# Sums for the seven-product form: x halves summed early, weights summed by transfers and one item ahead

## The chip, the cores and the metric

The kernel runs on one core of one Trainium2 chip. The metric is the device time of one execution in microseconds (us).

## The reference

Two decoder layers on a residual stream of 256 tokens by 2048, all in float32. Each layer has an attention, a cross attention into 256 memory tokens, and an MLP. Layer 0 uses differential attention; it is the stage that the change mostly touches.

```python
for i in range(DEPTH):                       # DEPTH = 2
    h = rms_norm(x, attn_norm[i])
    if i % 2 == 0:
        x = x + diff_attention(h, da_wqkv, da_lambda, da_subln, da_wo, cos_p, sin_p, lambda_init)
    else:
        x = x + mla_attention(h, ...)
    x = x + memory_cross_attention(rms_norm(x, cross_norm[i]), mem_h, ca_wq[i], ca_wkv[i], ca_wo[i])
    x = x + sq_relu_mlp(rms_norm(x, mlp_norm[i]), mlp_wup[i], mlp_wdown[i])   # square(relu(h @ wup)) @ wdown
return rms_norm(x, final_norm)

# diff_attention: q, k, v = split(h @ wqkv); q and k are rotated (cos, sin) in the first
# quarter of each head; per head two softmaxes p0, p1, a = p0 - lam * p1, o = a @ v
```

## The kernel before

**Products in halves.** Every float32 operand is split into a high part (the value rounded to the matmul's format) and a low part (value minus high part), and a product takes three matmuls: high·high, high·low, low·high. For the weights this happens on the fly. `load` brings 1 MB into a raw tile of 128x2048 (pool `wraw`, 7 slots) through SP's DMA queue. `split_pieces.next` then makes, for each half of the tile, `whi` by a cast on ScalarE (line 195) and `wlo` by a subtract on VectorE (line 196). The pool of these halves holds two raw tiles' worth, so a cast waits until TensorE has freed a slot. TensorE works on one half-tile of an ordinary item with 12 matmuls of 128x512, and so on through the list `plan`. `fill` keeps AHEAD = 4 items split ahead of `take`, and calls the `begin` of the next item already when it splits the one before. `hooks[n]` are run at the n-th `take`.

**The order** of the instructions on each engine is set by a scheduler with a cost model, within what is kept in program order (the queues, and the token "weights" on VectorE's splits and weight sums).

**Seven products.** Three of the query/key chunks of the diff layer (the groups 1 to 3, one class `Seven` for each in `diff_line`) and 14 blocks of the MLP (7 per layer, in `mlp_line`) multiply a 2x2 block matrix by a 2x2 block matrix in seven products p1 to p7 instead of eight. For it sums are needed on both sides. On the side of x these are s1 to s4 of x's quarters (`Forms.sums_of`, line 427 for the sum, `halves` at lines 396 and 397 for its high and low part). On the side of the weights they are built in the raw tiles, for each product in two halves x = 0, 1 of 1 MB:

- p5's tile is p1's tile plus block (0,1), by an add on VectorE (line 791) when p5's item begins.
- p7's tile is the tile of block (0,1) plus p3's tile (block (1,1)), by an add on VectorE (line 800) right behind p3's split.
- p6's tile is p7's plus block (0,0), and p4's is p6's plus block (1,0). Both are made by a transfer that accumulates, on POOL's queue (line 804), issued behind the split of the one before.

**The diff layer's start.** The first 8 items are the q and k chunks of group 0, of 24 matmuls per half tile. `x_pieces` (hooks 2 to 5) and the first loads make the high and low parts `acts` of the scaled x transposed. After q and k, `heads_T` evicts the results to `ev` tiles (line 486), rotates them on POOL with the tables `cos` and `sin` (lines 497 to 502), and TensorE transposes them (`mm<-identr,ev`, line 159). The tables are made on VectorE and ScalarE (lines 1006 to 1020). Only then `GivenForms` reads xT again (four transfers into two raw tiles), scales it on ScalarE (line 459), and makes the sums s1 to s4 for the products of the groups. Beside each group's products run the values' chunk, the output projection of the group before, and the attention of the group before as background tasks: `nmax` (541), `rsum` (548, 668), and `a` (674, 675) are parts of its softmax on VectorE.

Of the kernel before, what the change touches and what calls it, by code (L numbers as in the profile page):

```python
# [14 lines left out]
ALU = mybir.AluOpType  # L15
# [30 lines left out]
def trunk(ctx, tc, x, xT, mem, memT, positions, gcols, gfinal, lam_vecs, consts, W, out):  # L46
# [329 lines left out]
    class Forms(Stream):  # L376
# [37 lines left out]
        def sums(self):  # L414
            for key in [(t, h) for t in range(NT) for h in range(2)]:
                for task in self.forms[key].tasks:
                    yield task
            for x in range(2):
                self.sums_of(x, *(self.raw[t][:, 8 * h + 4 * x : 8 * h + 4 * x + 4] for t in range(NT) for h in range(2)))
                yield T_TURN  # L420

        def sums_of(self, x, a11, a12, a21, a22):
            for key, o, p, q, op in (
                ("s1", a22, a21, a22, ALU.subtract), ("s3", a21, a11, a21, ALU.subtract),
                ("s2", a22, a22, a11, ALU.subtract), ("s4", a12, a12, a22, ALU.add),
            ):
                nc.vector.tensor_tensor(o, p, q, op)  # L427
# [13 lines left out]
    class GivenForms(Forms):  # L441


        def __init__(self, src, units, gcol):
            self.src, self.units, self.gcol = src, units, gcol
            self.forms = {}
            task = Task(self.sums())
            for key in ("s1", "s2", "s3", "s4"):
                self.form(key).tasks.append(task)

        def sums(self):
            for x in range(2):
                rows = raw_tile().rearrange("p (k t) -> p k t", t=S)
                for h in range(2):
                    u = 2 * h + x
                    load(rows[:, 4 * h : 4 * h + 4], self.src[:, 4 * u : 4 * u + 4, :])
                    for i in range(4):
                        row = rows[:, 4 * h + i]
                        nc.scalar.activation(row, row, AF.Copy, scale=g[:, self.gcol + 4 * u + i : self.gcol + 4 * u + i + 1])
                    yield T_TURN  # L460
                self.sums_of(x, *(rows[:, 4 * h : 4 * h + 4, t * P : (t + 1) * P] for t in range(NT) for h in range(2)))
                yield T_SM

        def pieces(self, key):
            if key in self.forms:
# [297 lines left out]
    class Seven:  # L763
# [15 lines left out]
        def fetch(self, i, j, x):  # L779
            raw = raw_tile()  # L780
            load(raw, self.source(i, j, x))
            return raw

        def job(self, p, x):
            def begin():
                r = self.raw
                if p in self.B:
                    r[p, x] = self.fetch(*self.B[p], x)
                if p == "p5":
                    r[p, x], r["p7", x] = r["p1", x], self.fetch(0, 1, x)  # L790
                    in_turn(nc.vector.tensor_tensor(r[p, x], r[p, x], r["p7", x], ALU.add))  # L791

            def run():
                o = self.raw[p, x]
                split = split_pieces(o, 4 * CH, 2)
                for _ in range(2):
                    split.next()
                if p == "p3":
                    r = self.raw
                    in_turn(nc.vector.tensor_tensor(r["p7", x], r["p7", x], o, ALU.add))  # L800
                if p in self.ADDED:
                    after, block = self.ADDED[p]
                    self.raw[after, x] = o
                    add = nc.gpsimd.dma_start(o, self.source(*block, x), accum_op=ALU.add)  # L804
                    tc.keep_in_program_order(add)
                return split.halves

            run.begin = begin
            return run

        def items(self):
# [2 lines left out]
        def products(self, a, u, copied, out):  # L814
# [724 lines left out]
```

## Time and profile before

| | |
|---|---|
| median of 3 runs | 2243.6 us (2242.57 to 2243.88) |
| the profiled execution | 2243.97 us, its span 2242.1 us |
| TensorE busy | 2213.5 us, 99% of the span |
| VectorE, ScalarE, POOL busy | 1751.3, 1422.6, 185.3 us |
| mean granted clock of TensorE | 0.996 |
| matmuls | 10449 |

PE is TensorE (PEld its weight loads), DVE VectorE, ACT ScalarE, POOL GpSimd, SP the engine whose queue issues the loads. A row of a timeline gives start and duration in us, the engine, the line of the kernel, the operation, what it writes and reads, how many stand in the row, and in brackets the idle time ahead of it and what ended it. A row of the waits gives the sum, the number and the longest. A row of the windows gives for each engine the busy time and the number of instructions, then TensorE's granted clock, the share of the 16 DMA engines, and GB/s. q0 is the queue of POOL's transfers, q1 that of the others.

### The profile page before, as it was taken

What the parts mean: (1) busy time and instruction counts of PE and PEld (TensorE: products, weight loads), DVE (VectorE), ACT (ScalarE), POOL (GpSimd) and SP (SyncE); (2) the same over time, 40 slices, a digit from 0 to 9 for tenths busy, and PEclk for the clock granted to TensorE, in tenths of its full rate; (3) what the DMA queues carried; (4) which work ended last, traced back from release to release, by engine and by line L of the source; (5) the groups of instructions that cost most, each with busy time, mean ns of one, the idle gap of its engine ahead of it and who ended that gap; (6) DMA issues with size and microseconds to landing.
All of it is one profiled execution on the core that took longest, in us unless ns stands there. A gap on an engine that the chain in (4) does not pass through costs nothing.

```text
span 2242.1 us, 27565 instructions
## 1 busy us (share of the span) xinstructions
PE 2213.5 (99%) x10449; PEld 1841.6 (82%) x10449; DVE 1751.3 (78%) x1923; ACT 1422.6 (63%) x1921; POOL 185.3 (8%) x262
## 2 busy tenths in 40 slices
PE   9899999999999999999999999999999999999998
PEld 7678888888888888888889888888888888888886
DVE  6878888778888788788765766778887887887864
ACT  7766667666666666666655755566666666666664
POOL 0231120000000000000000311000000000000001
PEclk9999999999999999999999999999999999999999
DMA  9477787435887887877955234634679779779781
GB/s 381 159 238 227 238 241 257 164 132 208 258 257 242 253 257 241 252 255 235 274 171 186 102 141 160 253 132 151 235 236 274 242 234 276 241 235 274 238 291 57
DMA packets 75158, 498.78 MB, mean 222 GB/s; under 512 B 8592, under 2 KB 8976, under 8 KB 17680
## 3 DMA queue, kind: packets, MB, share of 16 engines
q1 hardware_dynamic: 64656, 424.66, 51.6%
q0 software_dynamic: 9792, 71.31, 16.8%
q8 instruction: 82, 1.34, 0.2%
q10 hardware_dynamic: 576, 1.05, 0.2%
q14 instruction: 52, 0.43, 0.0%
HBM read 494.88 MB, written 2.10 MB: 222 GB/s over the span
## 4 chain that ended last, share of the span: by engine, by line
PE 91%; DVE 5%; issue 1%; ACT 1%; DMA 1%; ACTq 0%; POOLq 0%; DVEq 0%
PE mm L155 61%; PE pr L155 23%; PE ax L155 3%; PE ax L159 2%; DVE wlo L196 2%; DVE raw L791 2%; ACT whi L195 1%; DMA raw<-in_da_wqkv_dram 1%; PE mm L159 1%; DVE unit L297 1%; DVE raw L800 0%; DVE unit L530 0%; DVE unit L397 0%; DVE raw L427 0%; DVE x L481 0%
## 5 line engine op out<-in xcount | busy, mean ns | idle before, releaser
L196 DVE TENSOR_TENSOR wlo<-raw,whi 128x1024 fp32r<-128x1024 f32 (+3 forms) x998 | 1199.0, 1211 | 411.1 <-ACT whi L195 374.7
L195 ACT CAST whi<-raw 128x1024 fp32r<-128x1024 f32 (+3 forms) x998 | 1038.5, 1042 | 692.8 <-PE mm L155 491.1
L155 PE MATMUL mm<-whi,unit 128*128 128x512 f32 (+3 forms) x4160 | 1324.0, 389 | 1.3 <-ACT unit L614 0.9
L155 PEld LDWEIGHTS mm<-whi,unit 128*128 128x128 f32 x4160 | 778.0, 188 | 153.4 <-ACT unit L614 1.3
L155 PE MATMUL mm<-wlo,unit 128*128 128x512 f32 (+3 forms) x2080 | 804.0, 387 | 6.5 <-DVE wlo L196 6.2
L155 PE MATMUL pr<-whi,unit 128*128 128x512 f32 x1904 | 614.2, 392 | 0.0
L155 PEld LDWEIGHTS mm<-wlo,unit 128*128 128x128 f32 x2080 | 391.8, 188 | 85.8 <-DVE wlo L196 14.4
L155 PEld LDWEIGHTS pr<-whi,unit 128*128 128x128 f32 x1904 | 358.6, 188 | 74.1
L155 PE MATMUL pr<-wlo,unit 128*128 128x512 f32 x952 | 372.3, 391 | 6.3 <-DVE wlo L196 6.1
L155 PEld LDWEIGHTS pr<-wlo,unit 128*128 128x128 f32 x952 | 179.4, 188 | 44.5 <-DVE wlo L196 8.3
L804 POOL DMA_DIRECT2D raw<-in_mlp_wup_dram x56 | 49.1, 876 | 1119.2 <-DVE wlo L196 1119.2
L481 DVE TENSOR_TENSOR x<-x,mm 128x512 f32<-128x512 f32 x152 | 99.8, 680 | 9.0 <-PE mm L155 8.5
L800 DVE TENSOR_TENSOR raw<-raw,raw 128x2048 f32<-128x2048 f32 x34 | 77.7, 2284 | 0.0
L791 DVE TENSOR_TENSOR raw<-raw,raw 128x2048 f32<-128x2048 f32 x34 | 77.6, 2283 | 0.0
L296 ACT CAST unit<-ax 128x512 fp32r<-128x512 f32 (+1 forms) x100 | 55.7, 570 | 26.1 <-PE ax L159 23.6
L336 POOL TENSOR_TENSOR rs<-rs,mhalf 128x1 f32<-128x1 f32 (+1 forms) x28 | 25.8, 925 | 556.0 <-DVE rs L335 556.0
L297 DVE TENSOR_TENSOR unit<-ax,unit 128x512 fp32r<-128x512 f32 (+1 forms) x100 | 65.3, 663 | 3.4 <-ACT unit L296 1.3
L543 ACT ACTIVATE p<-ax,nmax 128x256 f32<-128x256 f32 (+1 forms) x80 | 33.7, 429 | 24.7 <-DVE nmax L541 24.3
L330 ACT ACTIVATE junk<-x 128x512 bf16<-128x512 f32 x56 | 35.2, 628 | 9.4 <-DVE x L481 8.4
L155 PE MATMUL ax<-unit,unit 128*128 128x256 f32 (+1 forms) x240 | 37.2, 281 | 0.0
L155 PEld LDWEIGHTS ax<-unit,unit 128*128 128x128 f32 x240 | 34.3, 190 | 2.5
L155 PE MATMUL ax<-raw,unit 128*128 128x256 f32 (+1 forms) x240 | 35.3, 279 | 0.8 <-ACT unit L529 0.6
(182 smaller groups left out, 1020.9 us busy)
## 6 DMA issues: line engine op xcount, KB each, us to landing
raw<-in_mlp_wup_dram SPq DMA_DIRECT2D x128, 1024.0 KB, 5.0
raw<-in_mlp_wdown_dram SPq DMA_DIRECT2D x128, 1024.0 KB, 5.6
raw<-in_mlp_wup_dram POOLq DMA_DIRECT2D x56, 1024.0 KB, 9.3
raw<-in_da_wqkv_dram SPq DMA_DIRECT2D x45, 1024.0 KB, 7.0
raw<-in_da_wo_dram SPq DMA_DIRECT2D x16, 1024.0 KB, 5.5
raw<-in_ca_wkv_dram SPq DMA_DIRECT2D x16, 1024.0 KB, 5.0
raw<-in_mla_wo_dram SPq DMA_DIRECT2D x16, 1024.0 KB, 6.2
raw<-in_da_wqkv_dram POOLq DMA_DIRECT2D x12, 1024.0 KB, 11.0
```

What stands on the lines that cost most here:

```text
L155: return nc.tensor.matmul(o, stationary, moving, start=start, stop=stop, skip_group_check=not alone)
L159: nc.tensor.transpose(o, src, ident)
L195: nc.scalar.copy(hi, r)
L196: in_turn(nc.vector.tensor_tensor(lo, r, f32(hi), ALU.subtract))
L296: nc.scalar.copy(hi, src)
L297: nc.vector.tensor_tensor(dst[:, 1, :n, t * P : (t + 1) * P], src, f32(hi), ALU.subtract)
L330: nc.scalar.activation(junk[:, : src.shape[1]], src, AF.Square, accum_out=acc)
L481: nc.vector.tensor_tensor(xc, xc, ps, ALU.add)
L543: nc.scalar.activation(pr[:, i * w : (i + 1) * w], sb[:, i * w : (i + 1) * w], AF.Exp, bias=nmax[:, i : i + 1], accum_out=ssum[:, i : i + 1],)
L791: in_turn(nc.vector.tensor_tensor(r[p, x], r[p, x], r["p7", x], ALU.add))
L800: in_turn(nc.vector.tensor_tensor(r["p7", x], r["p7", x], o, ALU.add))
L804: add = nc.gpsimd.dma_start(o, self.source(*block, x), accum_op=ALU.add)
```

## The change

`GivenForms` is made at the seventh `take`, in the first chunks. It no longer reads xT: it adds the high and low parts of `acts` (an add of 128x1024 on VectorE, four in all, line 459 of the kernel after) into tiles of the pool of activation units, and it hands back between each two of the four sums, so that they are spread.

`Seven` splits its work into `begin` and `spent`. In the MLP p7's add now runs at p7's `begin`, which is one item ahead, and its result goes into p3's tile. `Chained`, new and used in the diff groups only, makes p7 by a transfer on POOL's queue that accumulates block (1,1) onto block (0,1), issued behind p5's split; so three of its four sums are made by transfers.

```diff
@@ class Forms
-                self.sums_of(x, *(self.raw[t][...] for t in range(NT) for h in range(2)))
+                views = [self.raw[t][:, 8 * h + 4 * x : 8 * h + 4 * x + 4] for t in range(NT) for h in range(2)]
+                for _ in self.sums_of(x, *views):
+                    pass
                 yield T_TURN
...
                 nc.vector.tensor_tensor(o, p, q, op)
                 self.halves(key, x, o)
+                yield
@@ class GivenForms
-        def __init__(self, src, units, gcol):
+        def __init__(self, units):
...
-                rows = raw_tile().rearrange("p (k t) -> p k t", t=S)
+                rows = f32(unit()).rearrange("p a k t -> p (a k) t")
                 for h in range(2):
-                    u = 2 * h + x
-                    load(rows[:, 4 * h : 4 * h + 4], self.src[:, 4 * u : 4 * u + 4, :])
-                    for i in range(4):
-                        row = rows[:, 4 * h + i]
-                        nc.scalar.activation(row, row, AF.Copy, scale=g[...])
+                    part = self.units[2 * h + x].tile
+                    nc.vector.tensor_tensor(rows[:, 4 * h : 4 * h + 4], f32(part[:, 0]), f32(part[:, 1]), ALU.add)
                     yield T_TURN
...
+                for _ in self.sums_of(x, *views):
+                    yield T_TURN
@@ class Seven
+        def begin(self, p, x):
+            r, other = self.raw, None
+            if p in self.B:
+                r[p, x] = self.fetch(*self.B[p], x)
+            elif p == "p5":
+                r[p, x], other = r.pop(("p1", x)), self.fetch(0, 1, x)
+                r["12", x] = other
+            elif p == "p7":
+                r[p, x], other = r.pop(("p3", x)), r.pop(("12", x))
+            if other is not None:
+                in_turn(nc.vector.tensor_tensor(r[p, x], r[p, x], other, ALU.add))
+
+        def added(self, o, block, x):
+            tc.keep_in_program_order(nc.gpsimd.dma_start(o, self.source(*block, x), accum_op=ALU.add))
+
+        def spent(self, p, x):
+            if p in self.ADDED:
+                after, block = self.ADDED[p]
+                self.raw[after, x] = self.raw[p, x]
+                self.added(self.raw[p, x], block, x)
...
-                if p == "p3":
-                    r = self.raw
-                    in_turn(nc.vector.tensor_tensor(r["p7", x], r["p7", x], o, ALU.add))
@@ new
+    class Chained(Seven):
+
+        def begin(self, p, x):
+            r = self.raw
+            if p in self.B:
+                r[p, x] = self.fetch(*self.B[p], x)
+            elif p == "p5":
+                r[p, x], r["p7", x] = r["p1", x], self.fetch(0, 1, x)
+                in_turn(nc.vector.tensor_tensor(r[p, x], r[p, x], r["p7", x], ALU.add))
+
+        def spent(self, p, x):
+            if p == "p5":
+                self.added(self.raw["p7", x], (1, 1), x)
+            super().spent(p, x)
@@ diff_line and the diff layer
-        seven = Seven("da_wqkv", 3 * (gi + 1)).items()
+        seven = Chained("da_wqkv", 3 * (gi + 1)).items()
...
+    hooks[7] = lambda: made.append(GivenForms(acts))
+    made = []
...
-    forms = GivenForms(xT, acts, G_ATTN)
...
-                item.of.products(forms, item.u, copied, produced)
+                item.of.products(made[0], item.u, copied, produced)
```

How the order on the engines moves is shown at four places. Numbers at the end of a name tell tiles apart.

VectorE in the first chunks. `unit_113`, `unit_139`, `unit_162` and `unit_185` are four of the units of `acts`, `raw_174` and `raw_210` weights of the first q chunk. Before:

```order
L196 TENSOR_TENSOR wlo_178<-raw_174,whi_177 128x1024
L196 TENSOR_TENSOR wlo_182<-raw_174,whi_181 128x1024
L324 SCALAR_TENSOR_TENSOR unit_185<-raw_186,g,unit_185 128x256 x4
L196 TENSOR_TENSOR wlo_213<-raw_210,whi_212 128x1024
L196 TENSOR_TENSOR wlo_217<-raw_210,whi_216 128x1024
```

After:

```order
L196 TENSOR_TENSOR wlo_178<-raw_174,whi_177 128x1024
L459 TENSOR_TENSOR unit_532<-unit_113 128x1024
L459 TENSOR_TENSOR unit_532<-unit_162 128x1024
L196 TENSOR_TENSOR wlo_182<-raw_174,whi_181 128x1024
L324 SCALAR_TENSOR_TENSOR unit_185<-raw_186,g,unit_185 128x256 x4
L429 TENSOR_TENSOR unit_532<-unit_532 128x4x128
L196 TENSOR_TENSOR wlo_213<-raw_210,whi_212 128x1024
L196 TENSOR_TENSOR wlo_217<-raw_210,whi_216 128x1024
```

Two of the four new adds and the first sum stand between the low halves now; the other sums follow in the next 40 rows.

ScalarE where the tables are made. `raw_411` is the last weight of the k chunk, `raw_522` the first of the values; `ev_478` (evicted earlier), `ev_490` are q's tiles, the two after k's. Before:

```order
L195 CAST whi_413<-raw_411 128x1024
L486 ACTIVATE ev_490<-mm_209,rq_441 128x512
L1016 ACT_TABLE_LOAD
L1016 ACTIVATE sin<-ang 128x96
L486 ACTIVATE ev_590<-mm_369,r_82_443 128x512
L195 CAST whi_417<-raw_411 128x1024
L486 ACTIVATE ev_602<-mm_370,r_83_445 128x512
L1020 ACTIVATE cos<-ang 128x96
L195 CAST whi_524<-raw_522 128x1024
L195 CAST whi_528<-raw_522 128x1024
```

After:

```order
L195 CAST whi_413<-raw_411 128x1024
L1047 ACTIVATE ls<-ls 128x2
L195 CAST whi_417<-raw_411 128x1024
L487 ACTIVATE ev_490<-mm_209,rq_441 128x512
L487 ACTIVATE ev_606<-mm_369,r_82_443 128x512
L487 ACTIVATE ev_618<-mm_370,r_83_445 128x512
L195 CAST whi_524<-raw_522 128x1024
L1037 ACT_TABLE_LOAD
L1037 ACTIVATE sin<-ang 128x96
L195 CAST whi_528<-raw_522 128x1024
L1041 ACTIVATE cos<-ang 128x96
```

The sine stands behind two more casts and two more evictions, and the cosine behind the cast `whi_528`. TensorE's order is the same there: `mm_208<-identr,ev_478` and `mm_209<-identr,ev_490` follow the last matmul of `whi_413`.

VectorE at the start of group 1: `raw_520` is p1's and then p5's first half, `raw_556` (`raw_566` after) the second, `raw_629` and `raw_681` (`raw_635` and `raw_675` after) block (0,1). Before:

```order
L791 TENSOR_TENSOR raw_556<-raw_556,raw_681 128x2048
L196 TENSOR_TENSOR wlo_685<-raw_520,whi_684 128x1024
L196 TENSOR_TENSOR wlo_689<-raw_520,whi_688 128x1024
L397 TENSOR_TENSOR unit_620<-raw_742,unit_620 128x512
L397 TENSOR_TENSOR unit_623<-raw_614,unit_623 128x512
L297 TENSOR_TENSOR unit_206<-mm_208,unit_206 128x4x128
L297 TENSOR_TENSOR unit_206<-mm_209,unit_206 128x4x128
L397 TENSOR_TENSOR unit_622<-raw_742,unit_622 128x512
L297 TENSOR_TENSOR unit_207<-mm_369,unit_207 128x4x128
L297 TENSOR_TENSOR unit_207<-mm_370,unit_207 128x4x128
L196 TENSOR_TENSOR wlo_729<-raw_556,whi_728 128x1024
L196 TENSOR_TENSOR wlo_733<-raw_556,whi_732 128x1024
```

After:

```order
L874 TENSOR_TENSOR raw_566<-raw_566,raw_675 128x2048
L196 TENSOR_TENSOR wlo_679<-raw_520,whi_678 128x1024
L196 TENSOR_TENSOR wlo_683<-raw_520,whi_682 128x1024
L196 TENSOR_TENSOR wlo_728<-raw_566,whi_727 128x1024
L196 TENSOR_TENSOR wlo_732<-raw_566,whi_731 128x1024
L297 TENSOR_TENSOR unit_207<-mm_369,unit_207 128x4x128
L297 TENSOR_TENSOR unit_207<-mm_370,unit_207 128x4x128
L196 TENSOR_TENSOR wlo_772<-raw_769,whi_771 128x1024
L196 TENSOR_TENSOR wlo_776<-raw_769,whi_775 128x1024
```

The sums between p5's low halves are gone. Further on the two adds of p7 with p3 (line 800) are gone too, and POOL issues two transfers onto `raw_635` and `raw_675` ahead of the two that it issued before.

VectorE in a block of the MLP: `raw_5573` and `raw_5634` (`raw_5557` and `raw_5617` after) are p3's halves, `raw_5474` and `raw_5503` (`raw_5458` and `raw_5487` after) block (0,1); the other raw tiles are ordinary items. Before:

```order
L196 TENSOR_TENSOR wlo_5605<-raw_5573,whi_5604 128x1024
L800 TENSOR_TENSOR raw_5474<-raw_5474,raw_5573 128x2048
L297 TENSOR_TENSOR unit_5319<-ax_5699,unit_5319 128x4x128
L196 TENSOR_TENSOR wlo_5639<-raw_5636,whi_5638 128x1024
L196 TENSOR_TENSOR wlo_5643<-raw_5636,whi_5642 128x1024
L196 TENSOR_TENSOR wlo_5659<-raw_5634,whi_5658 128x1024
L196 TENSOR_TENSOR wlo_5663<-raw_5634,whi_5662 128x1024
L800 TENSOR_TENSOR raw_5503<-raw_5503,raw_5634 128x2048
L196 TENSOR_TENSOR wlo_5686<-raw_5683,whi_5685 128x1024
L196 TENSOR_TENSOR wlo_5690<-raw_5683,whi_5689 128x1024
L196 TENSOR_TENSOR wlo_5725<-raw_5474,whi_5724 128x1024
```

After:

```order
L196 TENSOR_TENSOR wlo_5589<-raw_5557,whi_5588 128x1024
L297 TENSOR_TENSOR unit_5303<-ax_5682,unit_5303 128x4x128
L196 TENSOR_TENSOR wlo_5622<-raw_5619,whi_5621 128x1024
L196 TENSOR_TENSOR wlo_5626<-raw_5619,whi_5625 128x1024
L196 TENSOR_TENSOR wlo_5642<-raw_5617,whi_5641 128x1024
L196 TENSOR_TENSOR wlo_5646<-raw_5617,whi_5645 128x1024
L795 TENSOR_TENSOR raw_5557<-raw_5557,raw_5458 128x2048
L196 TENSOR_TENSOR wlo_5669<-raw_5666,whi_5668 128x1024
L196 TENSOR_TENSOR wlo_5673<-raw_5666,whi_5672 128x1024
L795 TENSOR_TENSOR raw_5617<-raw_5617,raw_5487 128x2048
L196 TENSOR_TENSOR wlo_5709<-raw_5557,whi_5708 128x1024
```

The first add stands four low halves later, the second two, right ahead of p7's first low half.

More of the change, by code (lines that the diff above doesn't have):

```diff
@@ L418, in sums @@
             for x in range(2):
-                self.sums_of(x, *(self.raw[t][:, 8 * h + 4 * x : 8 * h + 4 * x + 4] for t in range(NT) for h in range(2)))
+                views = [self.raw[t][:, 8 * h + 4 * x : 8 * h + 4 * x + 4] for t in range(NT) for h in range(2)]
+                for _ in self.sums_of(x, *views):
+                    pass
                 yield T_TURN
@@ L441, in trunk @@
     class GivenForms(Forms):
[L444 to L445 removed]
+        def __init__(self, units):
+            self.units = units
             self.forms = {}
@@ L452, in sums @@
             for x in range(2):
-                rows = raw_tile().rearrange("p (k t) -> p k t", t=S)
+                rows = f32(unit()).rearrange("p a k t -> p (a k) t")
                 for h in range(2):
-                    u = 2 * h + x
-                    load(rows[:, 4 * h : 4 * h + 4], self.src[:, 4 * u : 4 * u + 4, :])
-                    for i in range(4):
-                        row = rows[:, 4 * h + i]
-                        nc.scalar.activation(row, row, AF.Copy, scale=g[:, self.gcol + 4 * u + i : self.gcol + 4 * u + i + 1])
+                    part = self.units[2 * h + x].tile
+                    nc.vector.tensor_tensor(rows[:, 4 * h : 4 * h + 4], f32(part[:, 0]), f32(part[:, 1]), ALU.add)
                     yield T_TURN
-                self.sums_of(x, *(rows[:, 4 * h : 4 * h + 4, t * P : (t + 1) * P] for t in range(NT) for h in range(2)))
-                yield T_SM
+                views = [rows[:, 4 * h : 4 * h + 4, t * P : (t + 1) * P] for t in range(NT) for h in range(2)]
+                for _ in self.sums_of(x, *views):
+                    yield T_TURN
         def pieces(self, key):
@@ L782, in fetch @@
             return raw
-        def job(self, p, x):
-            def begin():
-                r = self.raw
[L787 to L791, printed above, removed]
+        def begin(self, p, x):
[16 more added lines that the diff above has]
+                self.added(self.raw[p, x], block, x)
+        def job(self, p, x):
             def run():
-                o = self.raw[p, x]
-                split = split_pieces(o, 4 * CH, 2)
+                split = split_pieces(self.raw[p, x], 4 * CH, 2)
                 for _ in range(2):
                     split.next()
-                if p == "p3":
[L799 to L805, printed above, removed]
+                self.spent(p, x)
                 return split.halves
-            run.begin = begin
+            run.begin = lambda: self.begin(p, x)
             return run
```

## The prediction

> **What bounds the kernel now.** I read the page first: the busy times and the DMA part.
>
> ```profile
> PE 2213.5 (99%) x10449; PEld 1841.6 (82%) x10449; DVE 1751.3 (78%) x1923; ACT 1422.6 (63%) x1921; POOL 185.3 (8%) x262
> ...
> q0 software_dynamic: 9792, 71.31, 16.8%
> ...
> raw<-in_mlp_wup_dram SPq DMA_DIRECT2D x128, 1024.0 KB, 5.0
> ...
> raw<-in_da_wqkv_dram SPq DMA_DIRECT2D x45, 1024.0 KB, 7.0
> ...
> raw<-in_da_wqkv_dram POOLq DMA_DIRECT2D x12, 1024.0 KB, 11.0
> ```
>
> TensorE works through the span and its matmuls are not changed, so all there is to win is 2242.1 − 2213.5 = 28.6 us of idle time, and the time in which its clock is lower. Where these lie I asked of the windows of the diff layer (columns after PE, PEld, DVE, ACT and POOL: granted clock, DMA share, GB/s), then of TensorE's waits from 0 to 350 us.
>
> ```profile
> 50.00:100.00 50.00, 44.07 (x198) 35.85 (x197) 42.45 (x51) 37.15 (x60) 12.65 (x24) 0.93 0.56 202
> ...
> 150.00:200.00 50.00, 47.48 (x224) 39.37 (x223) 46.17 (x52) 32.30 (x48) 12.85 (x9) 0.97 0.60 204
> 200.00:250.00 50.00, 50.00 (x242) 41.59 (x242) 39.65 (x56) 34.96 (x57) 12.96 (x23) 1.00 0.89 267
> 250.00:300.00 50.00, 48.67 (x230) 39.89 (x229) 48.52 (x59) 32.17 (x48) 4.63 (x8) 1.00 0.59 177
> ```
>
> ```profile
> PE pr L155 <- DVE wlo L196: 6.1, 4, 3.5
> PE mm L155 <- DVE wlo L196: 4.1, 3, 2.5
> PE ax L159 <- DVE a L675: 3.3, 2, 2.8
> ```
>
> Nearly every wait is for VectorE, though it is busy only 78% of the span. Three places hold it. TensorE's timeline, place A (start of group 1), then B, then C:
>
> ```profile
> 74.61 0.50 PE L155 MATMUL pr<-wlo,unit 128*128 128x512 f32 x1 [0.48 <-DVE wlo L196]
> ...
> 79.15 0.51 PE L155 MATMUL pr<-wlo,unit 128*128 128x512 f32 x1 [2.00 <-DVE wlo L196]
> ...
> 79.96 0.39 PE L155 MATMUL pr<-wlo,unit 128*128 128x512 f32 x1
> ...
> 80.64 0.39 PE L155 MATMUL pr<-wlo,unit 128*128 128x512 f32 x1
> ...
> 85.62 0.79 PE L155 MATMUL pr<-wlo,unit 128*128 128x512 f32 x1 [3.45 <-DVE wlo L196]
> ...
> 91.33 0.62 PE L155 MATMUL mm<-whi,unit 128*128 128x512 f32 x2
> ...
> 113.37 0.59 PE L159 MATMUL ax<-identr,a 128*128 128x128 f32 x2 [2.76 <-DVE a L675]
> ...
> 166.75 0.79 PE L155 MATMUL mm<-wlo,unit 128*128 128x512 f32 x1 [2.52 <-DVE wlo L196]
> ...
> 170.34 0.39 PE L155 MATMUL mm<-wlo,unit 128*128 128x512 f32 x1
> ```
>
> Three matmuls start within 0.68 us at full clock (79.96 to 80.64). From 85.62 to 91.33 only 13 start: 5.71 us instead of 13 × 0.227 = 2.95, so 2.76 us went to the lower clock. Behind C, nine matmuls take 3.59 us instead of 2.04: 1.55 us. So A costs 0.48 + 2.00 + 3.45 + 2.76 = 8.7 us, B 2.8, C 2.52 + 1.55 = 4.1.
>
> **The change, part by part.**
>
> *Sums of x halves early.* What VectorE does between 64 and 100 us, by shapes, and a window of its own:
>
> ```profile
> L397 DVE TENSOR_TENSOR unit<-raw,unit 128x512 fp32r<-128x512 f32 x8 | 5.5, 712 | 0.0
> L427 DVE TENSOR_TENSOR raw<-raw 128x512 f32<-128x512 f32 x8 | 5.4, 683 | 0.4 <-ACT raw L459 0.4
> ```
>
> ```profile
> 76.00:90.00 14.00, 8.54 (x32) 6.48 (x31) 14.00 (x16) 8.19 (x12) 0.00 (x0) 0.80 0.59 201
> ```
>
> At A VectorE never pauses: 14.00 of 14 us. The sums are 10.9 us of its work there and leave altogether; the backlog that ends in the three waits is 0.48 + 2.00 + 3.45 = 5.9 us, so A goes, and with it the lower clock: −8.7. The four xT loads (2 MB) and 16 scalings on ScalarE go too and free two weight slots there; with A already gone I cost them at nothing. If part of the last wait was for ScalarE's casts, an earlier raw tile serves that as well.
>
> The same sums now run in the first 60 us, beside the q and k chunks, plus four adds of 128x1024 elements, for which the low-half subtract of equal size (half of the 2.36 us below, 1.2) is the nearest row: 4.8 us. At the very start two of them stand ahead of a subtract; the row of before that holds it:
>
> ```profile
> 22.33 2.36 DVE L196 TENSOR_TENSOR wlo<-raw,whi 128x1024 fp32r<-128x1024 f32 x2 [0.99 <-ACT whi L195]
> ```
>
> VectorE had a pause of 0.99 us there against 2.4 us of added work, but its subtracts ran somewhat ahead of TensorE. I take 0.2 us lost (bounds 0 and 2.4 − 0.99 = 1.4).
>
> The price is later. The cosine and sine tables are made on ScalarE, and their steps now stand behind three evictions and two casts. Rows of ScalarE, VectorE, POOL's rotation and TensorE's transposes there:
>
> ```profile
> 55.16 0.28 ACT L1020 ACTIVATE cos<-ang 128x96 f32<-128x96 f32 x1
> ...
> 58.15 1.05 ACT L195 CAST whi<-raw 128x1024 fp32r<-128x1024 f32 x1 [1.72 <-PE mm L155]
> ...
> 59.23 1.33 DVE L196 TENSOR_TENSOR wlo<-raw,whi 128x1024 fp32r<-128x1024 f32 x1 [1.46 <-ACT whi L195]
> ...
> 59.15 0.32 POOL L501 TENSOR_TENSOR ev<-rope,rope 128x64 f32<-128x64 f32 x1
> 59.43 1.31 POOL L502 TENSOR_TENSOR ev<-rope,rope 128x64 f32<-128x64 f32 x1
> ...
> 60.62 1.03 PE L159 MATMUL mm<-identr,ev 128*128 128x128 f32 x8
> ```
>
> Before, the cosine ended at 55.44 and the second rotated tile at 59.43 + 1.31 = 60.74, just as TensorE came to it (60.62 to 61.4, eight transposes of two tiles). Now the cosine follows the cast that TensorE's freed slot releases at 58.15: 58.15 + 1.05 + 0.28 = 59.4, 4.0 us later. The chain behind it had 5.3 us (55.44 to 60.74). Ten operations at the unhindered step of 0.28 (59.15 to 59.43) take 2.8, with 1.0 more for each that meets a VectorE subtract (1.31 beside the one at 59.23). Two would be met, at 59.2 and 61.9: 59.4 + 2.8 + 2.0 = 64.2. TensorE waits for it from 60.85, less some 0.3 us for the first four transposes in between: 3.1 us. Bounds: no operation hindered, 59.4 + 2.8 − 60.85 − 0.3 = 1.1; the whole old chain, 59.4 + 5.3 − 60.85 − 0.3 = 3.6. Then the clock: 2.52 us idle at C lowered it, 2.76 at B did not, so nothing is lost or the 1.55 of C; I take 1.0, being nearer to C in a wait of 3. Sum here: +4.1.
>
> The Trainium skill ("TensorE: Matmul & The Clock Gate", section "HAM oscillation — how this bites in real kernels") allows idle gaps up to about 3.4 us. By that the clock would stay up here and the sum come out 1.0 us better. The trace does not agree at C, where 2.52 us was enough, so I keep the 1.0.
>
> *Weight sums of the diff groups by transfer.* Six adds of 2.28 us leave VectorE (two in each group). Rows of B's cause:
>
> ```profile
> 101.72 2.28 DVE L800 TENSOR_TENSOR raw<-raw,raw 128x2048 f32<-128x2048 f32 x1
> ...
> 112.97 0.60 DVE L675 SCALAR_TENSOR_TENSOR a<-p,rsum,a 128x128 f32<-128x128 f32 x2
> ```
>
> The operand that TensorE waited for was made at 112.97 behind 2 × 2.28 us of such adds in 20 us. They are more than the wait of 2.76, so B goes: −2.8. In VectorE's new order, parts of the softmax stand ahead of a low half instead; they are 0.5 us pieces, +0.3 (0 to 0.7). The group-2 and group-3 adds cover two smaller waits, 3.3 − 2.76 = 0.5 for the softmax operand and part of 4.1 − 2.52: −0.5.
>
> In their place POOL issues six transfers of 1 MB, ahead of its two others in each group. Their latency and the window:
>
> ```profile
> DMA to landing us min/median/max: 7.9/11.0/14.4
> ...
> 84.36 2.35 DVE L196 TENSOR_TENSOR wlo<-raw,whi 128x1024 fp32r<-128x1024 f32 x2
> ...
> 106.51 2.35 DVE L196 TENSOR_TENSOR wlo<-raw,whi 128x1024 fp32r<-128x1024 f32 x2
> ```
>
> The second half of p7 can go out when p5's split is done (84.36 + 2.35 = 86.7) and its cast is wanted 1.05 us before the subtract in 106.51's pair (at 107.7): 19.9 us, less the 2.76 of low clock that goes: 17. The longest latency seen is 14.4. So no wait, with 2.6 us to spare in group 1 and more behind it. What a transfer takes of the 16 DMA engines: 16.8% of 2242.1 / 68 = 5.5 us; in groups 2 and 3 it falls into the windows with shares of 0.60 and 0.59, not into that with 0.89. Cost nothing; if the cover is gone, see the third rival.
>
> C stays. Its cause is an old transfer, not a sum that moves:
>
> ```profile
> 136.39 0.90 POOL L804 DMA_DIRECT2D raw<-in_da_wqkv_dram  x1 [2.92 <-DVE rs L335]
> ...
> 151.98 1.23 DVE L196 TENSOR_TENSOR wlo<-raw,whi 128x1024 fp32r<-128x1024 f32 x1 [3.19 <-ACT whi L195]
> ...
> 162.08 2.28 DVE L791 TENSOR_TENSOR raw<-raw,raw 128x2048 f32<-128x2048 f32 x1
> ```
>
> p4's half, issued at 136.39, came 14.4 us later, VectorE idled 3.19 us and then had p5's sum (kept) in front of what TensorE wanted. Cost 0, bounds −4.1 (it goes) and +2 (the transfer takes as much longer as the spread above its median, in part).
>
> *MLP sums one item ahead.* Same adds, same length, in another place. Between 620 and 1260 us, with six of the seven such blocks of layer 0, TensorE waits for a subtract six times:
>
> ```profile
> PE mm L155 <- DVE wlo L196: 1.1, 6, 0.2
> ```
>
> These 0.18 us stand at p5's sum, which stays. At p7's there is no wait now; a new one of the same size for each of 28 adds would be 5.0 us, none is 0. I take 0: the slot held longer has loads of 5.0 us behind it that are issued items ahead.
>
> Sum: −8.7 + 0.2 + 4.1 − 2.8 + 0.3 − 0.5 = −7.4. The profiled execution took 2243.97, 0.4 above the median of 2243.6; so 2236.6 there, and 2236.2 as a median.
>
> **The rivals.**
>
> 1. *The rotation takes A's place.* If it meets three subtracts and each table step slips once more, TensorE waits 5 us in one piece and, as at A, loses 2.76: 7.8 instead of 4.1, time 2239.9; with the MLP's 5.0, 2245. Within 0.2%. For it: the rotation had no margin before (60.74 against 60.62). Against: the chain's old length bounds it at 3.6.
> 2. *Better than forecast.* The rotation meets nothing (1.1, no clock) and C goes, since the order around it is laid anew: −12.0 + 0.5 + 1.1 − 4.1 = −14.5, time 2229. For it: without 10.9 us of sums VectorE is less in arrears. Against: C's transfer is as late as before.
> 3. *Slower: p7's transfers come late.* They share the engines with the loads, which already take 7.0 us in this stage against 5.0 in the MLP. POOL's transfers go one behind the other; if p7's two take 20 us instead of at most 14.4, each of six halves is 3 us late in a window of 17, and with C's 1.55 for the clock that is 6 × 4.55 = 27: slower than before by 20, 2263. It decides from about 19 us (six times 2 us outweigh the gain even at full clock); one half per group late by 3 us and slowed (14 in all) would bring 2250. For it: a DMA share of 0.89 between 200 and 250 us. Against: 12 transfers, none above 14.4. The Trainium skill ("DMA: Bandwidth & Descriptors", section "Issuing engines are not separate DMA queues") says that all queues run on the same 16 engines, which the 7.0 against 5.0 bears out.
>
> **How the numbers follow.** A difference under 0.2% (4.5 us: 2239.1 to 2248.1) is about what a measurement here can't tell from none. Forecast, 2231 to 2239: 0.50. Better, below 2231: 0.17. Within 0.2%, mostly the first rival: 0.21. Slower, mostly the third: 0.12. So faster 0.67, same 0.21, slower 0.12. The range from 2227 to 2245 takes in the first two rivals and leaves out some 0.06 below and 0.14 above.
>
> **What would show it.** TensorE's waits between 70 and 92 us gone and the clock at 1.00 there; no wait for `a` near 105; a new wait of about 3 us near 61 us for the rotated tiles, with the cosine at about 59; C still there, some 6 us earlier; POOL's transfers of da_wqkv 18 instead of 12 and none above 15 us; the MLP's waits still some 0.18 at p5's sum. It is wrong if A keeps a wait (then ScalarE or the loads set it, not VectorE's sums), if TensorE waits for p7's casts, or if the MLP shows waits at every block.

## The result, and the profile after

The changed kernel takes 2237.3 us (median of 8 runs, 2233.9 to 2238.3), the kernel before 2243.8 (8 runs on the same chip): a ratio of 0.9968, with a 95% interval from 0.9957 to 0.9978. The forecast was 2236.2. The two fastest of the eight runs, 2233.9 and 2234.0, have a mean granted clock of 0.998, the profiled one, 2237.5, has 0.996; 0.002 of 2235 us is 4.5 us, so by this estimate the clock alone can make such a difference. The busy times and the transfers of the diff layer, from the page of the changed kernel:

```profile
PE 2213.1 (99%) x10449; PEld 1842.8 (82%) x10449; DVE 1742.5 (78%) x1921; ACT 1415.4 (63%) x1905; POOL 186.8 (8%) x268
...
raw<-in_da_wqkv_dram SPq DMA_DIRECT2D x45, 1024.0 KB, 9.2
raw<-in_da_wqkv_dram POOLq DMA_DIRECT2D x18, 1024.0 KB, 11.2
```

VectorE lost only 8.8 us of work, ScalarE 7.2; TensorE's busy time is the same. What moved are the waits. TensorE's waits up to 350 us:

```profile
PE mm L155 <- DVE wlo L196: 4.2, 3, 2.9
PE mm L159 <- POOL ev L503: 2.9, 2, 2.2
```

The products of the groups (`pr`) no longer wait at all, nor does the softmax operand `a`; new is a wait for POOL. The timeline of TensorE at the two places that are left, the rotation and C:

```profile
61.65 0.66 PE L159 MATMUL mm<-identr,ev 128*128 128x128 f32 x4 [0.75 <-POOL ev L503]
64.47 1.12 PE L159 MATMUL mm<-identr,ev 128*128 128x128 f32 x4 [2.16 <-POOL ev L503]
...
159.78 0.79 PE L155 MATMUL mm<-wlo,unit 128*128 128x512 f32 x1 [2.85 <-DVE wlo L196]
```

Windows of the changed kernel (granted clock third from the end): A's old place, the time behind the rotation, and the time behind C.

```profile
70.00:92.00 22.00, 22.00 (x108) 18.45 (x106) 18.73 (x16) 14.29 (x16) 1.90 (x2) 0.99 0.68 164
64.00:68.00 4.00, 3.53 (x11) 2.96 (x12) 0.69 (x1) 0.59 (x1) 3.84 (x14) 0.50 0.18 74
68.00:72.00 4.00, 4.00 (x14) 3.22 (x13) 0.22 (x1) 1.05 (x1) 0.01 (x1) 0.70 0.00 0
160.00:165.00 5.00, 5.00 (x12) 3.91 (x13) 5.00 (x4) 0.07 (x1) 5.00 (x1) 0.50 0.63 206
```

Both kernels have the same 10449 matmuls, so the start of the k-th in one trace can be set against the k-th in the other; their order differs only in a part of group 1. The difference (after minus before, in us) as it runs on:

| up to (time before) | difference | what lies between |
|---|---|---|
| 60.4 | +0.1 | the first loads, −0.3, and the early sums, +0.5 at 25 to 28 us |
| 73.1 | +6.3 | the rotation: 2.91 of waits, the other 3.2 put down to the slow clock |
| 102.1 | −3.2 | A: 9.4 gained |
| 126.9 | −7.3 | B and the small waits around it: 4.1 gained |
| 159.7 | −7.3 | |
| 173.1 | −5.5 | C: 1.8 lost |
| 295.1 | −6.5 | the softmax wait of 0.55 at 292: 1.0 gained |
| 2232.5 | −6.6 | all the rest, the whole MLP: 0.1 |

The spans differ by 2242.1 − 2235.4 = 6.7, which this accounts for.

### The profile page after: what moved, and what is told of

Read it like the earlier page. It is cut to its first block, busy times and chain, and to the rows that moved or that the text cites. A ratio compares the mean times of both kernels' runs of the same rounds, so it can differ in the third digit from the quotient of the medians.

```text
span 2235.4 us, 27536 instructions
## 1 busy us (share of the span) xinstructions
PE 2213.1 (99%) x10449; PEld 1842.8 (82%) x10449; DVE 1742.5 (78%) x1921; ACT 1415.4 (63%) x1905; POOL 186.8 (8%) x268
## 3 DMA queue, kind: packets, MB, share of 16 engines
q10 hardware_dynamic: 576, 1.05, 0.2%
## 4 chain that ended last, share of the span: by engine, by line
PE 91%; DVE 4%; ACT 1%; issue 1%; DMA 1%; POOL 0%; ACTq 0%; POOLq 0%; DVEq 0%
PE mm L155 61%; PE pr L155 24%; PE ax L155 3%; PE ax L159 2%; DVE wlo L196 2%; DVE raw L795 2%; DMA raw<-in_da_wqkv_dram 1%; ACT whi L195 1%; PE mm L159 1%; DVE unit L297 0%; DVE unit L531 0%; DVE raw L874 0%; DVE unit L324 0%; POOL rope L500 0%; DVE unit L711 0%
## 5 line engine op out<-in xcount | busy, mean ns | idle before, releaser
L795 DVE TENSOR_TENSOR raw<-raw,raw 128x2048 f32<-128x2048 f32 x56 | 127.9, 2284 | 0.0
L155 PEld LDWEIGHTS ax<-raw,unit 128*128 128x128 f32 x240 | 32.0, 190 | 2.4 <-ACT unit L530 1.0
```

The source lines that it names most:

```text
L155: return nc.tensor.matmul(o, stationary, moving, start=start, stop=stop, skip_group_check=not alone)
L795: in_turn(nc.vector.tensor_tensor(r[p, x], r[p, x], other, ALU.add))
```

## The experiments

**One part at a time.** `Joined` stands for the weight sums as they were before.

```diff
# sums of x early only
-  seven = Chained("da_wqkv", 3 * (gi + 1)).items()
+  seven = Joined("da_wqkv", 3 * (gi + 1)).items()
-  for item in Seven(f"mlp_wup{l}", 2 * b, b).items():
+  for item in Joined(f"mlp_wup{l}", 2 * b, b).items():
# transfers only: Chained kept, Joined in the MLP, GivenForms as before (reads xT, made after q and k)
# MLP only: Seven kept in the MLP, Joined in the groups, GivenForms as before
```

> Only the sums of x halves are made early; the diff groups and the MLP sum their weights as before (p7 by an add on VectorE behind p3's split). Theory (each part acts at its own place, as the two traces line up): the rotation near 61 us costs 6.1 us, place A gives 9.4 back, place B keeps its 2.8 us wait for the softmax operand and C its 2.5 plus slow clock; so 2243.8 + 6.1 - 9.4 = 2240.5. Rival 1 (A came from p7's adds as much as from the sums of x): a wait of over 1 us for a low half stays between 74 and 92 us and the time is above 2243. Rival 2 (the late tables are not due to the sums): TensorE does not wait at 61 us and the time is 2234.

> Only the diff groups make p7 by an accumulating transfer; the sums of x and the MLP as before. Theory: no wait at 61 us, A keeps its three waits (0.5 + 2.0 + 3.5 us) and slow clock, B goes (about -3.9), the wait of 0.55 us at 292 us goes (-1.0), C as before or up to 1.8 us worse: 2243.8 - 4.9 = 2238.9, up to 2240.7. Rival (B went because the sums of x left, not because of p7's adds): the 2.8 us wait for the softmax operand stays and the time is 2243 to 2245.

> Only the MLP's p7 add is made one item ahead, into p3's tile. Theory: the MLP's waits of 0.18 us stay at p5's sum and nothing else appears: 2243.8 within 0.5. Rival: the tile of block (0,1) given back sooner, or the add right ahead of p7's low half, moves each of 14 blocks by 0.2 us or more: 3 us or more either way.

| kernel | median, us | ratio to before, 95% interval |
|---|---|---|
| sums of x early only | 2238.6 | 0.9972 (0.9962 to 0.9983) |
| transfers only | 2240.1 | 0.9978 (0.9968 to 0.9987) |
| MLP only | 2244.3 | 0.9999 (0.9989 to 1.0008) |

Waits of TensorE with the sums of x early only:

```profile
61.51 0.66 PE L159 MATMUL mm<-identr,ev 128*128 128x128 f32 x4 [0.76 <-POOL ev L503]
64.32 1.11 PE L159 MATMUL mm<-identr,ev 128*128 128x128 f32 x4 [2.15 <-POOL ev L503]
109.04 0.65 PE L159 MATMUL ax<-identr,a 128*128 128x128 f32 x2 [1.32 <-DVE a L676]
161.47 0.50 PE L155 MATMUL mm<-wlo,unit 128*128 128x512 f32 x1 [2.88 <-DVE wlo L196]
```

and with the transfers only:

```profile
76.61 0.50 PE L155 MATMUL pr<-wlo,unit 128*128 128x512 f32 x1 [0.48 <-DVE wlo L196]
81.15 0.74 PE L155 MATMUL pr<-wlo,unit 128*128 128x512 f32 x1 [2.01 <-DVE wlo L196]
87.62 0.50 PE L155 MATMUL pr<-wlo,unit 128*128 128x512 f32 x1 [1.86 <-DVE wlo L196]
```

The sums of x alone take A away and bring the rotation's wait; the transfers alone leave A and take away B. So both main theories hold, and their rivals fall. Three points limit this:

- B is no clean case of one part. In the kernel with the MLP change only it is 2.81 us; the early sums alone leave 1.32 of it, the transfers alone nothing. What the sums win there the transfers would have won too. That is one reason why the gains overlap: the two ratios add up to 0.50%, the whole change gives 0.32%. Another is C's clock (below); the rest is inside the intervals.
- A's third wait is 1.86 us with the transfers only, against 3.45 before, but A is no cheaper. The wait ends at the same time, 2.0 us later in a trace that started 2.0 us later (87.62 and 85.62); TensorE only came to it later, since its clock was at half from 81.24 to 84.65 us, behind the second wait. The profiled execution of this kernel took 2243.25 us, 3.1 above its median; against before, 2.0 us of it are lost in the first 14 us, ahead of all that the change touches.
- With the early sums the four loads of xT and ScalarE's 16 scalings left too, and no kernel here parts them from the sums. The kernel with the sums later (below), in which part of A is back without these loads and scalings, speaks for the sums.

The third part did nothing that shows.

**A transfer too many.** In the diff groups p7's transfer is issued twice.

```diff
             if p == "p5":
                 self.added(self.raw["p7", x], (1, 1), x)
+                self.added(self.raw["p7", x], (1, 1), x)
```

> The changed kernel with p7's accumulating transfer issued twice in a row for each half in the diff groups, so p7's tile holds block (1,1) twice and the output is another. In the changed kernel p7's halves land 14.0 and 11.0 us (group 1), 8.5 and 6.0 us (group 2), and over 12 us (group 3) ahead of their casts. A second transfer adds about 9 us for the first half and 18 to 27 us for the second of each group. Theory (a late p7 is paid at p7's place, after that slack): TensorE waits for p7's low halves in groups 1 and 2, 12 to 25 us in all, time 2250 to 2265, while POOL's rotations queue behind. Rival (the loads give way or later items cover it): below 2243.

One run took 2273.0 us, 36 more than the changed kernel; more than was expected. Of the 36, 4 arose in the first 14 us, ahead of all that the edit touches. TensorE's longest waits stand at the places of p7, now for ScalarE's cast, which waits for the tile:

```profile
115.82 0.80 PE L155 MATMUL pr<-whi,unit 128*128 128x512 f32 x1 [8.64 <-ACT whi L195]
...
220.56 0.80 PE L155 MATMUL pr<-whi,unit 128*128 128x512 f32 x1 [8.35 <-ACT whi L195]
...
321.84 0.79 PE L155 MATMUL pr<-whi,unit 128*128 128x512 f32 x1 [4.99 <-ACT whi L195]
```

So what is late beyond the slack is paid: against the changed kernel the difference grows from 2 to 14 us in group 1, from 12 to 27 in group 2 and from 28 to 36 in group 3, with the slow clock behind each wait, and nothing later wins it back. The third rival's mechanism is real, and only its condition did not come about. Group 3 waits 4.99 us although it had over 12 us to spare, since POOL's own queue stands still until the first transfer onto a tile has landed (in group 3 it idled 18.6 us ahead of the second half's second transfer).

**The tables back to their place.** One kernel begins the tables one take earlier, the other the sums one take later.

```diff
# tables earlier
-    hooks[1] = lambda: load(const, consts)
+    hooks[1] = lambda: (load(const, consts), load(pos, positions), load(lamv, lam_vecs))
-    hooks[5] = lambda: x_pieces(4, 2)
+    hooks[5] = lambda: (tables(), x_pieces(4, 2))
# and no tables(), no loads of pos and lamv in first_norm
# sums later
-    hooks[7] = lambda: made.append(GivenForms(acts))
+    hooks[8] = lambda: made.append(GivenForms(acts))
```

> The changed kernel, with the cosine and sine tables begun one take earlier (tables() in the fifth hook, the positions and lambda vectors loaded with the constants at the first). Theory (the rotation's new wait near 61 us is only the late tables): both waits there (0.75 + 2.16 us) and the slow clock behind them go, 6.1 us in all, A stays gone, time 2237.3 - 6.1 = 2231. Rival 1 (VectorE's early sums hold the rotation in another way, through POOL's operations or the evictions): at least 2 us of waiting for the rotated tiles stays, time 2234 or more. Rival 2 (the earlier table steps push low halves late in the first chunks): a new wait before 55 us, gain under 4 us.

> The changed kernel, with the early sums begun at the eighth take instead of the seventh, so that the sums of the second half of x (about 7 us of VectorE's work) stand behind the tables, between 58 and 92 us. Theory: the tables keep their old place, the wait at 61 us goes (-6.1), and half of A's work is back on VectorE, with waits of 0 to 2 us at A: 2231 to 2234. Rival (A's backlog needs all of the sums to leave): A is back with over 4 us and the time is above 2235.

With the tables earlier the time is 2231.8 us, a ratio to before of 0.9939 (0.9925 to 0.9952); with the sums later 2231.6, 0.9941 (0.9929 to 0.9954). The first lost the rotation's waits altogether; all the waits over 0.5 us that it has between 15 and 350 us are C and its smaller twin in the next group:

```profile
155.72 0.50 PE L155 MATMUL mm<-wlo,unit 128*128 128x512 f32 x1 [2.88 <-DVE wlo L196]
249.50 0.50 PE L155 MATMUL mm<-wlo,unit 128*128 128x512 f32 x1 [0.79 <-DVE wlo L196]
```

The second pays part of A instead and, with another order around it, little of C:

```profile
77.03 0.50 PE L155 MATMUL pr<-wlo,unit 128*128 128x512 f32 x1 [0.80 <-DVE wlo L196]
80.97 0.49 PE L155 MATMUL pr<-wlo,unit 128*128 128x512 f32 x1 [1.40 <-DVE wlo L196]
156.62 0.50 PE L155 MATMUL mm<-wlo,unit 128*128 128x512 f32 x1 [0.77 <-DVE wlo L196]
```

So the late tables are what the early sums cost, and not VectorE's work as such: 2237.3 − 2231.8 = 5.5 us by the medians, and 6.5 by the ratios to before (0.9968 and 0.9939), since the two kernels ran on different chips.

**C: the late transfer or p5's sum.** One kernel loads p4 of group 1 plainly, the other leaves out p5's two adds of group 2.

```diff
# plain p4 (Chained, only where self.chunk == 3)
+            elif p == "p4" and self.chunk == 3:
+                r[p, x] = self.fetch(1, 0, x)
# no sum
-                in_turn(nc.vector.tensor_tensor(r[p, x], r[p, x], r["p7", x], ALU.add))
+                if self.chunk != 6:
+                    in_turn(nc.vector.tensor_tensor(r[p, x], r[p, x], r["p7", x], ALU.add))
```

> The changed kernel; p4 of group 1 is a plain load of block (1,0), issued items ahead on SP's queue, so the output is another. Theory 1 (C comes from the late accumulating transfer, 13.6 us in the changed kernel, behind which VectorE idles 2.9 us): VectorE does not idle near 144 us and the wait of 2.85 us at 160 us is under 0.5; time 2233 to 2235. Theory 2 (C comes from VectorE's work there, p5's sum in front): the wait stays above 2 us.

> The changed kernel without p5's two adds on VectorE in group 2, so the output is another. Theory 2 (C is p5's sum, 2.28 us, in front of the low half that TensorE wants): the wait at 160 us falls from 2.85 to about 0.6; time 2233 to 2235. Theory 1 alone (the late transfer, whatever stands behind it): the wait stays above 2 us. Both together give a fall in either kernel.

One run each: 2232.2 us for the plain load, 2233.5 without the sum. C's row in the one and in the other:

```profile
157.58 0.50 PE L155 MATMUL mm<-wlo,unit 128*128 128x512 f32 x1 [1.43 <-DVE wlo L196]
```

```profile
157.43 0.51 PE L155 MATMUL mm<-wlo,unit 128*128 128x512 f32 x1 [0.67 <-DVE wlo L196]
```

Neither theory holds alone: the wait falls in either kernel. Without the late transfer 1.4 of the 2.85 us go, without p5's sum 2.2, nearly its own length of 2.28; together they are more than the wait, so each covers part of the other. The times, one run each, are no measure of this: neither kernel had a slow clock behind C, and both had half as much of it behind the rotation as the changed kernel.

**p5's sum at its own turn.** If p5's sum in front of another item's low half is the harm, it could run behind that.

```diff
             def run():
+                self.own(p, x)            # p5: the add that begin made one item earlier
                 split = split_pieces(self.raw[p, x], 4 * CH, 2)
```

> The kernel with the early tables; in the diff groups p5's add on VectorE runs at p5's own turn, behind the split of the item before, instead of one item ahead. Theory (C is p5's sum in front of another item's low half, after VectorE fell behind by the late p4): the wait of 2.88 us near 156 us falls under 0.7 and that of 0.79 us near 250 us goes; p5's own low half has 5.4 us of TensorE's work before it against 2.3 + 1.0 + 1.2 us, so nothing new there; time 2231.8 - 3 to 3.5 = 2228.5. Rival (the wait only moves on to p5): a wait of 2 us or more for p5's first low half, time 2231 to 2233.

> As the kernel before it, with p5's add at its own turn in the MLP's 14 blocks too. Theory: the MLP's waits of 0.18 us stand at p5's sum in front of another item, so they go: 12 to 14 times 0.18 = 2.2 to 2.5 us less, 2226. Rival (in the MLP VectorE has less room between p1 and p5): waits for p5's low halves of 0.3 us or more in each block, 2231 or more.

In the groups alone it takes 2240.3 us (0.9983 of before, 0.9974 to 0.9992), in the MLP too 2263.8 (1.0084, 1.0070 to 1.0097). C fell to 0.67, as the theory said, but as the rival said the wait moved on to p5. It stands at p5's second half, not the first, and costs more than the rival had it. Group 2:

```profile
156.70 0.50 PE L155 MATMUL mm<-wlo,unit 128*128 128x512 f32 x1 [0.67 <-DVE wlo L196]
162.76 0.50 PE L155 MATMUL pr<-wlo,unit 128*128 128x512 f32 x1 [0.33 <-DVE wlo L196]
167.85 0.50 PE L155 MATMUL pr<-whi,unit 128*128 128x512 f32 x1 [1.93 <-ACT whi L195]
169.11 0.50 PE L155 MATMUL pr<-wlo,unit 128*128 128x512 f32 x1 [0.76 <-DVE wlo L196]
```

p5's second half has add, cast and low half in a row behind the first half's split, 2.28 + 1.05 + 1.2 us, and they do not end in time. In the MLP six blocks wait 3.7 us for p5's casts and 4.6 for its low halves, 1.4 us a block. That is what a sum one item ahead is worth here: 8.5 us in three groups, with C's gain already taken off, and 23.5 more in 14 blocks, of which the traces show 19.2 in the MLPs; the rest lies in the start and the clock.

**p4's transfer earlier.** The ordinary item behind p2 goes behind p6 in group 1's line.

```diff
-        for n in (1, 1, 1, 1, 1, 2, 1) if gi else (0, 1, 0, 1, 1, 2, 0):
+        for n in (1, 1, 1, 1, 1, 2, 1) if gi else (0, 1, 0, 1, 0, 3, 0):
```

> The kernel with the early tables; in group 1's line the ordinary item behind p2 stands behind p6 instead, so that p4's transfers have 5.4 us more before they are wanted and p6's have 5.4 us less. In the changed kernel p6's halves landed 5.6 and 5.8 us before their casts, p4's 0.9 and 0.4. Theory (C needs the late p4): VectorE does not idle near 140 us, the wait of 2.88 us at C is under 1.5, as with a plain load (1.43), and p6 is just in time: 2231.8 - 1.5 = 2230.3. Rival (the wait moves to p6's transfers): a wait of over 1 us for p6's halves, time 2232 or more.

2228.1 us, a ratio to before of 0.9932 (0.9918 to 0.9945): the lowest median of all, 9.2 us under the change as given by the medians and 8.1 by the ratios. The interval overlaps with that of the earlier tables alone, but in the traces 3.4 us of the gain over that kernel lie at C: a wait shorter by 1.46 and no slow clock behind it. C's wait is what the plain load left, and there is none for p6:

```profile
152.53 0.50 PE L155 MATMUL mm<-wlo,unit 128*128 128x512 f32 x1 [1.42 <-DVE wlo L196]
```

## Why the prediction was right

The sum was −7.4; the traces differ by 6.6 to 6.7, the medians by 6.5. The places and the mechanisms came out as forecast. That the sum came out within 1 us is in part luck: A, B and the smaller waits gave about 3 us more than forecast, the rotation and C took about 4 more. Its steps, by the table of differences:

- *The first chunks:* +0.2 forecast, +0.1 measured, which is an accident of two parts: −0.3 before 14 us and +0.5 at 25 to 28 us, behind the first of the new sums. The kernel with only the sums of x early lost nothing there. Between single executions the first 14 us alone differ by −0.4 to +2.8 us from before, whatever the kernel.
- *A:* −8.7 forecast, −9.4 measured. The sums of x were its cause, as the kernels with one part each show.
- *The rotation:* +4.1 forecast, +6.1 measured. The wait was worked out well: 3.1 forecast, 0.75 + 2.16 = 2.91 measured. Cosine, the two stretched operations of POOL and the ready tile in the changed kernel:

```profile
59.23 0.27 ACT L1041 ACTIVATE cos<-ang 128x96 f32<-128x96 f32 x1
```

```profile
59.58 1.18 POOL L498 TENSOR_TENSOR rope<-ev,cos 128x64 f32<-128x64 f32 x1 [0.68 <-ACT cos L1041]
...
62.11 1.35 POOL L500 TENSOR_TENSOR rope<-ev,cos 128x64 f32<-128x64 f32 x1
...
64.09 0.32 POOL L503 TENSOR_TENSOR ev<-rope,rope 128x64 f32<-128x64 f32 x1
```

  The cosine ended at 59.50 (59.4 forecast), two operations met a subtract, and the tile was ready at 64.41 (64.2 forecast). Mis-sized was the term for the clock: 1.0 taken, 3.2 measured by difference.
- *B:* −2.8 + 0.3 forecast, −4.1 measured. The waits of 0.2 us around it went too, and the softmax pieces ahead of a low half cost nothing. The smaller waits of groups 2 and 3: −0.5 forecast, −1.0 measured, at 292 us.
- *p7's transfers:* nothing forecast, nothing measured, but with a wrong reason. I let them start behind p5's split and left 2.6 us to spare. They start as soon as p5's add has read block (0,1), so group 1 had 11 us. In group 2 it was 6: POOL issued late and both at once, so that the second landed behind the first and took 18.4 us instead of "none above 15":

```profile
DMA to landing us min/median/max: 7.9/11.2/18.4
```

- *C:* 0 forecast, +1.8 measured. Its wait grew from 2.52 to 2.85; the rest is clock again, 3.0 us lost instead of 1.55, and as the next lines show that is chance.
- *The MLP:* 0 forecast, −0.1 measured in the whole rest.

What decides between nothing and 3 us of slow clock the traces show. In each of them the granted clock is 1.00 or 0.50, and the stretches at 0.50, but for one at the program's end, last 3.41 us or a multiple of it; in any one trace they start whole multiples of 3.413 us apart (before: 84.49 and 166.41 us, 24 × 3.413). So the clock follows a grid that does not move with the kernel's waits. What counts is how much of one stretch of the grid TensorE idles. Windows laid on the grid (the first number behind the length is TensorE's busy time, the third from the end the clock): B before, two stretches; then B in the kernel with the MLP change only; then C before, each with the stretch behind it.

```profile
108.38:111.79 3.41, 2.23 (x10) 1.48 (x8) 3.41 (x8) 2.29 (x3) 1.58 (x2) 1.00 0.59 84
111.79:115.21 3.42, 1.84 (x9) 1.46 (x10) 3.42 (x8) 0.37 (x1) 0.00 (x0) 1.00 1.06 220
```

```profile
108.28:111.69 3.41, 0.77 (x4) 0.31 (x2) 3.41 (x8) 1.55 (x2) 0.87 (x1) 1.00 1.03 173
111.69:115.11 3.42, 3.25 (x9) 2.60 (x10) 2.97 (x8) 0.37 (x1) 0.00 (x0) 0.50 1.01 208
```

```profile
162.99:166.41 3.42, 1.24 (x6) 0.70 (x4) 3.42 (x4) 2.41 (x4) 3.34 (x5) 1.00 0.00 0
166.41:169.82 3.41, 3.07 (x7) 2.48 (x8) 3.41 (x3) 0.10 (x1) 3.41 (x1) 0.50 0.28 43
```

B is the same wait in the first two kernels, 2.76 and 2.81 us. Before, an edge of the grid cut it into 1.18 and 1.58 us, and the clock stayed; in the other kernel 2.64 us of it fell into one stretch, and the next was at half. The places by this measure (the last column by the same differences as above, good to some 0.4 us):

| place and kernel | wait, us | idle in one stretch and in the next | stretches at half behind | lost to the clock, us |
|---|---|---|---|---|
| B, before | 2.76 | 1.18, 1.58 | 0 | 0 |
| B, MLP only | 2.81 | 2.64, 0.16 | 1 | 1.4 |
| C, before | 2.52 | 2.18, 0.34 | 1 | 1.55 |
| C, sums of x early only | 2.88 | 0.48, 2.39 | 1 | 1.6 |
| C, tables earlier | 2.88 | 0.20, 2.68 | 1 | 2.1 |
| C, changed kernel | 2.85 | 2.18, 0.68 | 2 | 3.0 |
| the rotation, plain p4 | 2.9 in two | 0.25, 2.66 | 1 | 2.1 |
| the rotation, changed kernel | 2.91 in two | 1.98, 0.94 | 2 | 3.2 |
| C, p4 earlier in the line | 1.42 | 1.42 | 0 | 0.1 |

Counted over the traces of all 13 kernels, from 20 us on: of some 8300 stretches of the grid at full clock, all 20 in which TensorE idled 1.95 us or more were followed by one at half, three of the five with 1.73 to 1.90 us, and none with 1.57 or less. A stretch at half was followed by another one where TensorE idled 0.81 us or more in it, and never at 0.53 or less. This is why one wait of 2.85 us loses 1.6 us and another 3.0: the second reached across an edge into the first stretch at half. Where the grid stands differs from trace to trace (edges at 4.3 to 7.0 us from the start), so for one place in one kernel it is chance.

The Trainium skill ("TensorE: Matmul & The Clock Gate", section "What's actually happening") has the clock set by free-running windows of 3413 ns; that agrees with these stretches. Its rule to have no idle gaps above about 3.4 us ("HAM oscillation — how this bites in real kernels") is too lenient by these traces: 1.95 us of idle time in one stretch was always enough.

## What to carry to other kernels

Moving work off a busy stretch of an engine is worth the wait that ends there, and what it pushes back in the stretch that takes it up has to be followed to its last consumer: here the tables were pushed by 4 us, and beginning them earlier was worth nearly as much as the whole change. Where TensorE idles some 2 us or more within one stretch of 3.41 us, count 1.5 to 3 us of slow clock behind it; where it idles under 1.6, count none. For a wait of 2.85 us that is a matter of chance: it escapes only if an edge cuts it into two parts of under about 1.8 us each, which by these counts is so for some 0.75 of 3.41 us, about one place in five (an estimate). A sum on VectorE needs its place one item ahead: at its own turn it cost 0.7 us (MLP, 1.4 a block) to 1.4 us (groups, 8.5 / 6, C's gain taken off) for each half. An accumulating transfer may be late by its slack, and what it is late beyond that is paid.

## What the runs showed of the hardware

An operation of POOL that takes 0.32 us took 7.03 while VectorE went through subtracts and adds of two raw tiles or halves without a pause; it ended 0.18 us after the last of them. Just ahead of it POOL ran at its usual step, beside an add of VectorE that reads one operand from where TensorE writes (`ax`). Timeline of POOL, then of VectorE, in the changed kernel:

```profile
157.54 0.31 POOL L499 TENSOR_TENSOR rope<-u,sin 128x64 f32<-128x64 f32 x1
...
158.49 7.03 POOL L502 TENSOR_TENSOR u<-rope,rope 128x64 f32<-128x64 f32 x1
165.48 0.32 POOL L503 TENSOR_TENSOR u<-rope,rope 128x64 f32<-128x64 f32 x1
165.75 1.81 POOL L798 DMA_DIRECT2D raw<-in_da_wqkv_dram  x2
```

```profile
157.32 1.28 DVE L297 TENSOR_TENSOR unit<-ax,unit 128x512 fp32r<-128x512 f32 x2
158.52 2.34 DVE L196 TENSOR_TENSOR wlo<-raw,whi 128x1024 fp32r<-128x1024 f32 x2
160.79 2.28 DVE L874 TENSOR_TENSOR raw<-raw,raw 128x2048 f32<-128x2048 f32 x1
162.99 2.35 DVE L196 TENSOR_TENSOR wlo<-raw,whi 128x1024 fp32r<-128x1024 f32 x2
```

The two transfers of p7 stood in POOL's queue behind it: the first could have gone out at 157.4, when p5's add had read its tile, and went out at 165.75. The Trainium skill ("GPSIMD Engine Reference", section "1. Specifications") says that POOL shares its SBUF interfaces with VectorE and contends with VectorE's instructions of two SBUF inputs; this agrees, and shows that POOL can be held over five such instructions in a row. Transfers that stand in POOL's queue behind its arithmetic are then late by as much, here by 8 us.
